# Samples' attention scores on VectorE alone, with their softmax queued behind the prompt's scores

## The chip, the cores and the metric

The kernel runs on one core of a Trainium2 chip. The metric is the device time of one execution in microseconds (us); runs of the kernel before are summed up by their median. Besides them there is one profiled execution with its trace. The engines are named as in the profile: PE (TensorE, matrix products; PEld its weight loads), DVE (VectorE), ACT (ScalarE), POOL (GpSimd) and SP (SyncE, which here only issues transfers). Each engine works through its own queue in order and waits at an instruction whose inputs or buffers aren't ready.

## The reference

One inference step of a decoder layer for a prompt of 1024 rows and 8 samples of 4 rows each, with shared weights, 1024 features wide:

```
p = rmsnorm(x) @ w_in  ->  h, c, b | u, v | q | gate logits gA, gB, gM
y_a = b * conv3(c * h)
y_b = u * spatial_gate(layernorm(v))
y_m = softmax(q k^T / 16) v          (4 heads of 256, 256 memory tokens)
x = x + (sig(gA) y_a + sig(gB) y_b + sig(gM) y_m) @ w_o
x = x + (silu(g) * a) @ w_down,      a, g = conv3(rmsnorm(x) @ w_up) + bias
```

and a last norm. For the prompt all rows share one memory, whose keys and values come from the step itself. Each of the 8 samples has a memory of its own in a cache: 256 keys and 256 values for each head. So the samples' scores are, in each head, 32 rows of q (8 samples of 4), each against the 256 keys of its own sample. This part is what the change touches.

## The kernel before

All 1056 rows lie as columns, features on the partitions. Each weight tile of 128 output features is a *unit*: it is loaded by SP (`load_unit`, L177), split into a rounded high part by ACT (`wh`, L199) and a low rest by DVE (`wl`, L201), and multiplied in three passes (L222 to L224) over three *chunks* of 352 columns. A chunk is 8 x 3 matmuls into one PSUM bank of three (`bank("mm")`), and its evacuation (`evac`) empties the bank with ACT or DVE.

The order is written out by hand. Smaller work stands as a list of functions in the queue `aux`. In every chunk `weave()` is called twice, in its middle and behind its evacuation; each call stands for a *piece* of the large product and emits as many items of `aux` as `pace(n)` spreads over n pieces. What an item emits goes into the queues of its engines at that place.

The attention runs head by head. `plan[h]` lists a head's units: q twice, then h, c, b, h, c, b (the convolution branch; c's evacuation has DVE's convolution at L1127, L316, L318, b's one DVE product at L1137), then u, gB, gA and gM in pairs. At the third unit the list of `att_items(h)` is put into `aux` and paced over 62 pieces; it has 83 items, and heads 1 to 3 get four more (two loads six places before the end, two uses behind it). Head 0 has the rest of the spatial gate's items in the queue ahead of it. At gM the queue is emptied.

The list before, in order:

- `rows`: the 32 rows of q are transposed by PE (L834), copied to `qr` and stored to DRAM (`q_d`). `fetch_q` reads four rows of a sample back on all 128 partitions; `fetch` loads keys or values of two samples from the cache. Buffers come from `fs` (nine slots, F32) and `rs` (eight slots), handed out in turn.
- for each sample `bb` and half of its keys `mt`: `product` (POOL, L852) multiplies the four rows with 128 keys into a buffer of 4 x 256, and `total` (DVE, L865), emitted ahead of the next product, sums it to four columns of `sc`.
- then `masked` (POOL clears two masks), `kv_load` (SP loads the prompt's keys and values of the head), `softmax` (PE transposes `sc` at L874; DVE and ACT normalise), `masked_p`; then for each sample `parts` (its values split) and `against` (its matmuls).
- the prompt at the end: `kv_split` (ACT the high part, L974, DVE the low part, L975), and `score`, `turn_p`, `value` for four tiles of 256 rows: score matmuls at L988 to L990, the maximum at L993, the exponential at L996, transposes at L1013.

The items change places by their order in this list alone; engines and waits follow from it.

Of the kernel before, what the change touches and what calls it, by code (L numbers as in the profile page):

```python
# [9 lines left out]
F32 = mybir.dt.float32  # L10
# [5 lines left out]
P = 128  # L16
# [15 lines left out]
class Slots:  # L32
    """Fixed SBUF buffers of one dtype, handed out in turn."""
# [22 lines left out]
def layer_step(ctx: ExitStack, tc: tile.TileContext, I, O):  # L56
# [52 lines left out]
    def pace(n):  # L109
        """The queued work is to be spread over the next n pieces."""  # L110
        slots_left[0] = n
        due[0] = 0.0

    def until(ready):
        """What is queued, up to the work that makes ready() true."""
        while not ready():
            aux.popleft()()
# [65 lines left out]
    def split_lows():  # L183
        """The low parts, queued apart from the high ones that they wait for."""
        while lows:
            lows.pop()()
# [57 lines left out]
    def rsqrt(ms, out, tmp, n):  # L244
        """out = ms ** -0.5, the square root's table refined by one Newton step."""
        nc.scalar.activation(out=out[:n], in_=ms[:n], func=AF.Sqrt)
        nc.vector.reciprocal(out=out[:n], in_=out[:n])
        nc.vector.tensor_tensor(out=tmp[:n], in0=out[:n], in1=out[:n], op=ALU.mult)
        nc.vector.scalar_tensor_tensor(
            out=tmp[:n], in0=tmp[:n], scalar=-0.5, in1=ms[:n], op0=ALU.mult, op1=ALU.mult  # L250
        )
        nc.vector.scalar_tensor_tensor(
            out=out[:n], in0=tmp[:n], scalar=1.5, in1=out[:n], op0=ALU.add, op1=ALU.mult
        )

    def column_norm(c, g, sums):
        """S's chunk c of columns times their inverse root mean square and g, split into zhi and zlo."""
        r = slice(c * CH, (c + 1) * CH)
        ms, t, y = (small.tile([P, 3], F32, name=n, tag=n, bufs=2) for n in ("ms3", "tmp3", "y3"))
        tmp = fs.get()  # L260
        rows = []

        def total():
            sums(ms)
            nc.vector.tensor_scalar(out=ms, in0=ms, scalar1=1.0 / D, scalar2=EPS, op0=ALU.mult, op1=ALU.add)
            rsqrt(ms, y, t, P)

        def spread():
            b = bank()
            for i in range(3):  # L270
                n = PIECES[3 * c + i][1]
                mmul(
                    b[:, i * P : i * P + n], lhsT=y[:n, i : i + 1].to_broadcast([n, P]), rhs=ident[:n, :n],
                    start=True, stop=True,
                )
            rows.append(b)

        def scale(f):
            def go():
                z = tmp[:, (f % 3) * CH : (f % 3 + 1) * CH]  # L280
                nc.vector.scalar_tensor_tensor(
                    out=z, in0=S[:, f, r], scalar=col(g + f), in1=rows[0][:, :CH], op0=ALU.mult, op1=ALU.mult
                )
                nc.scalar.copy(out=zhi[:, f, r], in_=z)
                if f:
                    low(f - 1)
                if f == 7:
                    low(7)
                    fs.put(tmp)
            return go  # L290

        def low(f):
            z = tmp[:, (f % 3) * CH : (f % 3 + 1) * CH]
            eng = nc.gpsimd if f % 2 else nc.vector
            eng.tensor_tensor(out=zlo[:, f, r], in0=z, in1=f32(zhi[:, f, r]), op=ALU.subtract)  # L295

        nc.gpsimd.memset(ms, 1.0)
        return total, spread, [scale(f) for f in range(8)]
# [4 lines left out]
    def segments(c, hb, o):  # L303
        """(a chunk's columns of o, the function of a tap that gives hb's columns)."""
        t0, t1 = c * CH, min((c + 1) * CH, NP)
        segs = [(o[:, t0:t1], lambda k: hb[:, t0 + k : t1 + k])]
        if c == 2:
            hs = hb[:, 1026:HB].rearrange("p (b x) -> p b x", x=6)
            segs.append((o[:, NP:T].rearrange("p (b x) -> p b x", x=4), lambda k: hs[:, :, k : k + 4]))
        return segs  # L310

    def conv(c, hb, o, w0, step, first=True):
        """A chunk of the causal depthwise convolution of three taps."""
# [22 lines left out]
    def hb_parts(c, hb, ps):  # L336
        """(destination in hb, source in ps) of a chunk's columns."""
# [17 lines left out]
    def tail_rows(src, i0, cnt, prompt, sample):  # L355
        """Rows of the convolution states from their columns, for cnt tiles of channels."""
# [10 lines left out]
    with tc.manual_schedule():  # L367
# [87 lines left out]
        def x_prep(c, copy):  # L455
            """The sums of the squares, by rows; the turns, by columns; the norm's steps."""
# [34 lines left out]
        # mem's parts: 8 x 256 columns in two buffers each  # L491
        class Two:
            """[P, 8, 256] over two buffers."""
# [43 lines left out]
        def prep_sg2(g):  # L537
            def go():
# [7 lines left out]
                # the first 4 x 4 block, transposed, once for each sample on the diagonal  # L546
# [152 lines left out]
        def keep_warm(n):  # L699
            """Products that nothing reads: the tensor engine's clock is halved while it idles."""  # L700
            b = bank("acc")
            for _ in range(n):
                mmul(b[:, :P], lhsT=ident, rhs=ident, start=True, stop=True)
# [59 lines left out]
        kv = {}  # L763

        def turn_k(q):
            """Four tiles of the keys' columns, transposed."""
# [55 lines left out]
        att = {}  # L822

        def att_items(h):
# [5 lines left out]
            # the samples' scores: each row of q, on all partitions, times its memory's keys  # L830
            def rows():
# [3 lines left out]
                qr = small.tile([32, 256], F32, name="qr", tag="qr", bufs=1)  # L835
                nc.scalar.copy(out=qr, in_=b[:32, :256])
                nc.scalar.dma_start(out=q_d[h], in_=qr)
# [10 lines left out]
            def product(bb, mt):  # L848
                def go():
                    t = v3(att["st", bb // 2], 4, 256)  # L850
                    pr = att["pr", bb, mt] = fs.get()
                    nc.gpsimd.tensor_tensor(  # L852
                        out=v3(pr, 4, 256), in0=v3(att["qb", bb], 4, 256),
                        in1=t[:, 2 * (bb % 2) + mt, :].unsqueeze(1).to_broadcast([P, 4, 256]), op=ALU.mult,
                    )
# [4 lines left out]
                return go  # L860

            def total(bb, mt):
                def go():
                    pr = att.pop(("pr", bb, mt))
                    nc.vector.tensor_reduce(  # L865
                        out=att["sc"][:, mt, 4 * bb : 4 * bb + 4], in_=v3(pr, 4, 256), axis=AX.X, op=ALU.add
                    )
                    fs.put(pr)
                return go
# [15 lines left out]
            # their values: all their rows of a head at once, each against its own memory  # L885
# [60 lines left out]

            def folded_o():
                ym[:] = [fs.get(), fs.get()]
# [12 lines left out]
            # the prompt  # L961
# [83 lines left out]
            last = no  # L1045
            for bb in range(8):
                for mt in range(2):
                    items += [lambda last=last, do=product(bb, mt): (last(), do())]
                    last = total(bb, mt)
                    if mt and bb + 2 < 8:  # L1050
                        items.append(fetch_q(bb + 2))
                    else:
                        items.append(no)
                if bb % 2 and bb // 2 + 2 < 4:
                    items.append(fetch(kc, bb // 2 + 2))
            items += [last, masked, fetch(vc, 0), kv_load, softmax, fetch(vc, 1), no, masked_p]
# [6 lines left out]
            items += [against(7), copied, kv_split, folded_o]  # L1063
            items += [score(0), score(1), turn_p(0), score(2), turn_p(1), value(0), score(3), turn_p(2)]
            items += [value(1), turn_p(3), value(2), value(3)]
            return items

# [224 lines left out]
        def down(w, q, j0, nk, fi, r):  # L1292
            """One tile of features of w_down's product over nk tiles of j, added to S."""
# [59 lines left out]
        def finish(a0, a1, end):  # L1353
            """The rows of the columns from a0 to a1: their turns, one by one, then the last steps."""
# [114 lines left out]
```

## Time and profile before

| | |
|---|---|
| time, median of 3 runs | 1937.43 us (1936.9 to 1938.99) |
| span of the profiled execution, first to last instruction | 1939.3 us |
| busy: PE / PEld | 1889.9 / 1865.7 us |
| busy: DVE / ACT / POOL | 1062.2 / 660.5 / 284.7 us |
| mean granted PE clock | 0.988 |

The runs list no time for the profiled execution outside its span. A busy time is a union of spans. A row of a group reads: line, engine, operation, output <- inputs, shape, count | busy us, mean ns of one | idle us of the engine just before them, and what ended it. A row of waits reads: who waited <- for whom: us in total, times, longest. A row of the timeline: start us, length us, engine, line, operation; several of a kind in a row are merged (x2). A row of a stage table: stretch, its length, then busy us and instructions (x) of PE, PEld, DVE, ACT and POOL, the granted clock, the DMA engines' share and GB/s.

### The profile page before, as it was taken

The page shows a single profiled execution, that of the slowest core. Times are in us where ns is not written, and L with a number is a line of the kernel's source. Part 1 is how long each engine was busy: PE and PEld are TensorE (multiplying, and loading weights), DVE is VectorE, ACT ScalarE, POOL GpSimd, SP SyncE. Part 2 cuts the span into 40 slices and gives each one's busy share as a digit, 9 for nine tenths or more (in the row PEclk, how much of TensorE's full clock was granted, in tenths as well). Part 3 has the DMA queues.
Part 4 walks back from the last instruction along what each step waited for, and adds up shares of the span by engine and source line. Part 5 has one row for each costly group of instructions (what it writes and reads, how often), then busy time and mean ns, then how long its engine had stood idle before and what let it go on. Part 6 is the DMA issues. An engine that isn't in the chain of part 4 may idle for free.

```text
span 1939.3 us, 28762 instructions
## 1 busy us (share of the span) xinstructions
PE 1889.9 (97%) x11844; PEld 1865.7 (96%) x11844; DVE 1062.2 (55%) x1826; ACT 660.5 (34%) x1253; POOL 284.7 (15%) x386
## 2 busy tenths in 40 slices
PE   8999998999899989999999999999999999999998
PEld 8988998999899989999899999999999999999997
DVE  4476675336733383327636257636636546546666
ACT  6654312411152113421154135414414314222443
POOL 2231153005300260007100221000000000000000
PEclk9999999999999999999999999999999999999999
DMA  8636144124311252124314201111111111111123
GB/s 259 199 107 214 60 141 132 33 66 135 106 36 45 92 155 62 42 70 140 98 35 138 74 12 34 56 51 49 46 44 44 45 44 44 57 44 44 46 77 134
DMA packets 204848, 160.43 MB, mean 83 GB/s; under 512 B 5477, under 2 KB 191405, under 8 KB 204717
## 3 DMA queue, kind: packets, MB, share of 16 engines
q1 hardware_dynamic: 194660, 144.76, 24.6%
q10 hardware_dynamic: 10057, 13.84, 2.1%
q8 instruction: 93, 1.52, 0.3%
q14 instruction: 38, 0.31, 0.1%
HBM read 144.98 MB, written 13.59 MB: 82 GB/s over the span
## 4 chain that ended last, share of the span: by engine, by line
PE 81%; DVE 10%; issue 4%; ACT 2%; POOL 2%; DMA 1%; ACTq 0%; DVEq 0%; SPq 0%; POOLq 0%
PE mm L222 25%; PE mm L223 25%; PE mm L224 25%; DVE fs L318 3%; DVE sc L865 2%; POOL fs L852 1%; DVE wl L201 1%; DVE fs L316 1%; PE acc L919 1%; ACT wh L199 1%; DVE fs L1127 0%; DMA ws<-in_w_in 0%; PE mm L803 0%; PE aux L989 0%; PE aux L990 0%
## 5 line engine op out<-in xcount | busy, mean ns | idle before, releaser
L222 PE MATMUL mm<-zhi,wh 128*128 128x352 f32 x2880 | 939.8, 326 | 8.6 <-DVE fs L1137 8.3
L223 PE MATMUL mm<-zlo,wh 128*128 128x352 f32 x2880 | 935.4, 325 | 1.0 <-POOL zlo L295 1.0
L224 PE MATMUL mm<-zhi,wl 128*128 128x352 f32 x2880 | 934.9, 325 | 0.0
L222 PEld LDWEIGHTS mm<-zhi,wh 128*128 128x128 f32 x2880 | 546.3, 190 | 11.0 <-issue 7.3
L223 PEld LDWEIGHTS mm<-zlo,wh 128*128 128x128 f32 x2880 | 545.8, 190 | 1.6 <-POOL zlo L295 1.6
L224 PEld LDWEIGHTS mm<-zhi,wl 128*128 128x128 f32 x2880 | 545.9, 190 | 0.1
L201 DVE TENSOR_TENSOR wl<-ws,wh 128x1024 fp32r<-128x1024 f32 x181 | 234.9, 1299 | 141.5 <-ACT wh L199 141.3
L199 ACT CAST wh<-ws 128x1024 fp32r<-128x1024 f32 x182 | 190.9, 1051 | 352.2 <-PE mm L223 298.3
L318 DVE SCALAR_TENSOR_TENSOR fs<-fs,vec,fs 128x352 f32<-128x352 f32 (+2 forms) x416 | 236.5, 582 | 98.2 <-ACT fs L1280 88.9
L852 POOL TENSOR_TENSOR fs<-fs,fs 128x1024 f32<-128x1024 f32 x64 | 161.8, 2550 | 238.6 <-DMA fs<-q_d 204.9
L222 PE MATMUL mm<-rs,wh 128*128 128x352 f32 (+3 forms) x528 | 172.0, 326 | 2.1 <-DVE S L1302 2.1
L223 PE MATMUL mm<-rs,wh 128*128 128x352 f32 (+3 forms) x528 | 171.1, 324 | 0.0
L224 PE MATMUL mm<-rs,wl 128*128 128x352 f32 (+3 forms) x528 | 170.9, 324 | 0.0
L1302 DVE TENSOR_TENSOR S<-mm,S 128x352 f32<-128x352 f32 (+3 forms) x144 | 75.1, 524 | 124.0 <-PE mm L224 123.8
L222 PEld LDWEIGHTS mm<-rs,wh 128*128 128x128 f32 x528 | 99.1, 188 | 3.2 <-ACT fs L360 1.7
L330 POOL COPY tail_f<-fs 128x2 f32<-128x2 f32 x40 | 9.9, 247 | 624.7 <-ACT fs L1279 624.7
L223 PEld LDWEIGHTS mm<-rs,wh 128*128 128x128 f32 x528 | 99.3, 188 | 0.5 <-DVE rs L1269 0.3
L224 PEld LDWEIGHTS mm<-rs,wl 128*128 128x128 f32 x528 | 99.0, 188 | 0.2
L1279 ACT COPY fs<-mm 128x352 f32<-128x352 f32 (+2 forms) x176 | 62.1, 380 | 91.9 <-PE mm L224 85.2
L865 DVE TENSOR_REDUCE sc<-fs 128x4 f32<-128x1024 f32 x64 | 77.3, 1213 | 17.7 <-POOL fs L852 17.7
L1280 ACT ACTIVATE fs<-mm,vec 128x352 f32<-128x352 f32 x132 | 86.5, 656 | 0.0
L1160 DVE TENSOR_TENSOR sig<-sig,fs 128x352 f32<-128x352 f32 x48 | 25.2, 525 | 111.1 <-ACT sig L1147 111.1
(236 smaller groups left out, 1631.3 us busy)
## 6 DMA issues: line engine op xcount, KB each, us to landing
ws<-in_w_in SPq DMA_DIRECT2D x88, 512.0 KB
ws<-in_w_up SPq DMA_DIRECT2D x44, 512.0 KB
fs<-q_d SPq DMA_DIRECT2D x32, 512.0 KB
ws<-in_w_down SPq DMA_DIRECT2D x30, 512.0 KB
fs<-in_cache_mem_k SPq DMA_DIRECT2D x16, 512.0 KB
fs<-in_cache_mem_v SPq DMA_DIRECT2D x16, 512.0 KB
xT_d<-S ACTq DMA_DIRECT2D x3, 1408.0 KB
S<-xT_d ACTq DMA_DIRECT2D x6, 704.0 KB
```

The lines of the kernel that those rows point to most:

```text
L199: nc.scalar.copy(out=hi, in_=t)
L201: lows.append(lambda: eng.tensor_tensor(out=lo, in0=t, in1=f32(hi), op=ALU.subtract))
L222: mmul(ps, lhsT=wh, rhs=xh, start=first, stop=False)
L223: mmul(ps, lhsT=wh, rhs=xl, start=False, stop=False)
L224: mmul(ps, lhsT=wl, rhs=xh, start=False, stop=last)
L318: nc.vector.scalar_tensor_tensor(out=dst, in0=src(k), scalar=col(w0 + k * step), in1=dst, op0=ALU.mult, op1=ALU.add)
L852: nc.gpsimd.tensor_tensor(out=v3(pr, 4, 256), in0=v3(att["qb", bb], 4, 256), in1=t[:, 2 * (bb % 2) + mt, :].unsqueeze(1).to_broadcast([P, ...
L865: nc.vector.tensor_reduce(out=att["sc"][:, mt, 4 * bb : 4 * bb + 4], in_=v3(pr, 4, 256), axis=AX.X, op=ALU.add)
L1160: nc.vector.tensor_tensor(out=t, in0=t, in1=src[:, r], op=ALU.mult)
L1279: nc.scalar.copy(out=dst, in_=src)
L1280: nc.scalar.activation(out=o[:, r], in_=ps, func=AF.Identity, scale=col(CFW + 88 + i), bias=col(CFB + i))
L1302: nc.vector.tensor_tensor(out=S[:, f, r], in0=ps, in1=S[:, f, r], op=ALU.add)
```

## The change

`product` no longer runs on POOL. It emits four DVE instructions, one for each row of q, that multiply 256 elements of the row with 128 keys and sum along the row in the same instruction; the sum goes to one column of `sc`, the product itself to `qr`, enlarged to 128 partitions, which nobody reads after its store. `total` and its buffers are gone.

The list is in another order. `kv_load` stands after the seventh sample's products; behind the last product come `kv_split`, `started` (it takes the two output buffers that `folded_o` took) and the prompt's tiles; `softmax` stands among these, ten items behind the last product; `fetch` of the values, `masked` and `masked_p` follow, then the samples' values as before. It has 83 items again. Other parts of the diff only remove comments.

```diff
-                qr = small.tile([32, 256], F32, name="qr", tag="qr", bufs=1)
-                nc.scalar.copy(out=qr, in_=b[:32, :256])
-                nc.scalar.dma_start(out=q_d[h], in_=qr)
+                att["qr"] = qr = small.tile([P, 256], F32, name="qr", tag="qr", bufs=1)
+                nc.scalar.copy(out=qr[:32], in_=b[:32, :256])
+                nc.scalar.dma_start(out=q_d[h], in_=qr[:32])
...
             def product(bb, mt):
+
                 def go():
                     t = v3(att["st", bb // 2], 4, 256)
-                    pr = att["pr", bb, mt] = fs.get()
-                    nc.gpsimd.tensor_tensor(
-                        out=v3(pr, 4, 256), in0=v3(att["qb", bb], 4, 256),
-                        in1=t[:, 2 * (bb % 2) + mt, :].unsqueeze(1).to_broadcast([P, 4, 256]), op=ALU.mult,
-                    )
+                    q = v3(att["qb", bb], 4, 256)
+                    for i in range(4):
+                        at = 4 * bb + i
+                        nc.vector.tensor_tensor_reduce(
+                            out=att["qr"], in0=q[:, i, :], in1=t[:, 2 * (bb % 2) + mt, :], scale=1.0, scalar=0.0,
+                            op0=ALU.mult, op1=ALU.add, accum_out=att["sc"][:, mt, at : at + 1],
+                        )
...
-            def total(bb, mt):
-                def go():
-                    pr = att.pop(("pr", bb, mt))
-                    nc.vector.tensor_reduce(
-                        out=att["sc"][:, mt, 4 * bb : 4 * bb + 4], in_=v3(pr, 4, 256), axis=AX.X, op=ALU.add
-                    )
-                    fs.put(pr)
-                return go
...
+            def started():
+                ym[:] = [fs.get(), fs.get()]
+
             def folded_o():
-                ym[:] = [fs.get(), fs.get()]
...
-            last = no
             for bb in range(8):
                 for mt in range(2):
-                    items += [lambda last=last, do=product(bb, mt): (last(), do())]
-                    last = total(bb, mt)
-                    if mt and bb + 2 < 8:
-                        items.append(fetch_q(bb + 2))
-                    else:
-                        items.append(no)
+                    items.append(product(bb, mt))
+                    items.append(fetch_q(bb + 2) if mt and bb + 2 < 8 else no)
                 if bb % 2 and bb // 2 + 2 < 4:
                     items.append(fetch(kc, bb // 2 + 2))
-            items += [last, masked, fetch(vc, 0), kv_load, softmax, fetch(vc, 1), no, masked_p]
+                if bb == 6:
+                    items.append(kv_load)
+            items += [kv_split, started, score(0), score(1), turn_p(0), score(2), turn_p(1), value(0), score(3), turn_p(2)]
+            items += [softmax, value(1), turn_p(3), fetch(vc, 0), value(2), value(3), masked, fetch(vc, 1), masked_p]
             for bb in range(8):
...
-            items += [against(7), copied, kv_split, folded_o]
-            items += [score(0), score(1), turn_p(0), score(2), turn_p(1), value(0), score(3), turn_p(2)]
-            items += [value(1), turn_p(3), value(2), value(3)]
+            items += [against(7), copied, no, folded_o]
             return items
```

## The prediction

> **What bounds the kernel now.** I read the page first: TensorE (PE) is busy nearly throughout, so only time in which it waits, or runs at a lowered clock, can be won.
>
> ```profile
> span 1939.3 us, 28762 instructions
> PE 1889.9 (97%) x11844; PEld 1865.7 (96%) x11844; DVE 1062.2 (55%) x1826; ACT 660.5 (34%) x1253; POOL 284.7 (15%) x386
> L852 POOL TENSOR_TENSOR fs<-fs,fs 128x1024 f32<-128x1024 f32 x64 | 161.8, 2550 | 238.6 <-DMA fs<-q_d 204.9
> L865 DVE TENSOR_REDUCE sc<-fs 128x4 f32<-128x1024 f32 x64 | 77.3, 1213 | 17.7 <-POOL fs L852 17.7
> ```
>
> Then the waits in the four heads (244 to 1100 us), by engine and line, and one of them in the timeline:
>
> ```profile
> PE aux L874 <- DVE sc L865: 19.9, 8, 3.8
> 509.38 0.39 PE L874 MATMUL aux<-ident,sc 128*32 128x128 f32 x1 [3.84 <-DVE sc L865]
> 511.64 0.40 PE L874 MATMUL aux<-ident,sc 128*32 128x128 f32 x1 [1.87 <-DVE sc L865]
> L222 PE MATMUL mm<-zhi,wh 128*128 128x352 f32 x1532 | 501.9, 328 | 8.3 <-DVE fs L1137 8.3
> ```
>
> PE waits twice per head: at softmax's transposes (L874), for the last sums of the samples' scores, and once earlier, for a PSUM bank that VectorE (DVE) empties late. What these cost, clock included, is read from the stage table: 480 to 500 us is undisturbed, the other rows hold the stalls.
>
> ```profile
> 290.00:300.00 10.00, 8.34 (x52) 8.08 (x51) 8.47 (x12) 1.05 (x1) 7.13 (x4) 1.00 0.72 218
> 305.00:318.00 13.00, 7.93 (x33) 7.19 (x33) 8.16 (x11) 3.08 (x5) 6.28 (x4) 0.74 0.72 224
> 472.00:478.00 6.00, 3.85 (x24) 3.59 (x23) 6.00 (x8) 1.05 (x1) 3.93 (x2) 1.00 0.83 264
> 480.00:500.00 20.00, 20.00 (x127) 20.00 (x126) 16.36 (x13) 2.91 (x4) 17.82 (x9) 1.00 0.53 157
> 504.00:516.00 12.00, 6.29 (x31) 5.71 (x30) 9.15 (x13) 1.84 (x3) 3.58 (x3) 0.72 0.54 173
> 684.00:694.00 10.00, 7.83 (x39) 7.57 (x39) 9.93 (x14) 1.50 (x2) 6.68 (x3) 0.83 0.64 186
> 720.00:732.00 12.00, 7.50 (x34) 6.68 (x33) 7.41 (x14) 2.03 (x4) 1.10 (x2) 0.72 0.56 175
> 898.00:908.00 10.00, 7.83 (x40) 7.57 (x39) 9.93 (x14) 1.39 (x2) 6.50 (x4) 0.83 0.59 182
> 934.00:946.00 12.00, 7.39 (x33) 6.65 (x31) 7.10 (x13) 1.84 (x3) 1.34 (x2) 0.72 0.56 174
> ```
>
> Undisturbed, PE starts 127/20 = 6.35 matmuls per us, so a chunk (24) takes 3.78 us and a piece (12) 1.89 us. The four softmax windows hold 33, 31, 34 and 33 where 49 us would hold 311: (311 - 131)/6.35 = 28.3 us lost, of which 49 - 29.1 = 19.9 is idleness and 8.4, about 2 per head, is the granted clock (0.72 to 0.74). The four bank windows hold 155 where 36 us would hold 229: 11.6 us. Together **39.9 us** can be won, no more.
>
> Why DVE is late: beside GpSimd (POOL) its convolution steps are slow. The first five rows are the heads, the next three 1120 to 1300 us, where no product runs:
>
> ```profile
> L201 DVE TENSOR_TENSOR wl<-ws,wh 128x1024 fp32r<-128x1024 f32 x64 | 86.5, 1351 | 57.5 <-ACT wh L199 57.4
> L318 DVE SCALAR_TENSOR_TENSOR fs<-fs,vec,fs 128x352 f32<-128x352 f32 x30 | 33.5, 1116 | 1.6
> L318 DVE SCALAR_TENSOR_TENSOR fs<-fs,vec,fs 128x320 f32<-128x320 f32 x16 | 30.1, 1879 | 0.6
> L318 DVE SCALAR_TENSOR_TENSOR fs<-fs,vec,fs 128x32 f32<-128x32 f32 x16 | 4.0, 252 | 0.6
> L1161 DVE TENSOR_TENSOR S<-S,sig 128x352 f32<-128x352 f32 x48 | 25.2, 525 | 1.6
> ...
> L318 DVE SCALAR_TENSOR_TENSOR fs<-fs,vec,fs 128x352 f32<-128x352 f32 x36 | 20.8, 584 | 11.6 <-ACT fs L1280 10.8
> L201 DVE TENSOR_TENSOR wl<-ws,wh 128x1024 fp32r<-128x1024 f32 x13 | 15.9, 1221 | 6.9 <-ACT wh L199 6.9
> L318 DVE SCALAR_TENSOR_TENSOR fs<-fs,vec,fs 128x320 f32<-128x320 f32 x18 | 9.9, 550 | 3.5 <-ACT fs L1280 3.2
> ```
>
> 30 x (1116 - 584) + 16 x (1879 - 550) + 64 x (1351 - 1221) ns = 45.5 us of DVE time, 11.4 a head, is such slowing.
>
> **The change, part by part.** *Removed:* POOL's 16 products a head, the slowing, and DVE's 16 sums (19.4 us a head at 1213 ns). *Added:* 64 multiply-and-sum instructions a head of 128x256, all on DVE. Before shows none. Nearest rows, and how instructions follow one another:
>
> ```profile
> L676 DVE TENSOR_TENSOR S<-aux,S 128x256 f32<-128x256 f32 x32 | 13.6, 425 | 1.1
> L1374 DVE TENSOR_TENSOR ms<-ss 128x1 f32<-128x1 f32 x8 | 1.2, 154 | 1.5 <-ACT fs L1369 1.5
> 499.25 0.51 DVE L1127 TENSOR_TENSOR fs<-mm,fs 128x352 f32<-128x352 f32 x1
> 499.80 0.40 DVE L316 TENSOR_SCALAR fs<-fs,vec 128x352 f32<-128x352 f32 x1
> 500.24 1.21 DVE L318 SCALAR_TENSOR_TENSOR fs<-fs,vec,fs 128x352 f32<-128x352 f32 x2
> 501.36 1.22 DVE L865 TENSOR_REDUCE sc<-fs 128x4 f32<-128x1024 f32 x1
> 6.44 1.06 ACT L464 ACTIVATE S<-fs 128x1024 f32<-128x1024 f32 x1
> 7.41 0.19 ACT L464 ACTIVATION_READ_ACCUMULATOR S<-fs 128x1 f32 x1
> 7.66 1.06 ACT L464 ACTIVATE S<-fs 96x1024 f32<-96x1024 f32 x1
> ```
>
> An independent successor starts 0.09 us before its predecessor's end (501.36 against 501.45), a dependent one 0.04 after it. All 64 write the same tile qr, which nobody reads; ACT's three squares at L464 do the same with S, and there each starts only when the one before, with its accumulator read, is over: 7.66 - 6.44 = 1.22, or 0.16 us beyond the main duration. So for the time t from start to start: at the least 0.425 - 0.09 = 0.34 (nothing waits, no read); 0.46 (dependent, no read); 0.34 + 0.154 + 0.04 = 0.53 (a read like DVE's smallest operation); 0.425 + 0.16 = 0.585 (ACT's overhead). I take **t = 0.50**, between the two middle ones, and keep 0.34 and 0.585 for the range.
>
> [...]
>
> *What the new work delays.* DVE works in order. In the stretch of the products it also has to empty PE's banks, split the weights, and now, right after the last product, split the prompt's keys (kv_split), for which the prompt's first score matmul waits. Head 1, from these starts:
>
> ```profile
> 439.36 0.38 PE L834 MATMUL aux<-ident,qs 128*32 128x128 f32 x2
> 450.82 1.23 DVE L201 TENSOR_TENSOR wl<-ws,wh 128x1024 fp32r<-128x1024 f32 x1 [10.43 <-ACT wh L199]
> 446.18 4.78 POOL L852 TENSOR_TENSOR fs<-fs,fs 128x1024 f32<-128x1024 f32 x2 [64.57 <-DMA fs<-q_d]
> 441.71 0.81 SPq L843 DMA_DIRECT2D fs<-q_d  x2
> ```
>
> The first product stands behind the weight split that ends at 452.05 (q has landed by 446.18, so that wait is hidden by 5.9 us). Behind it, up to the end of kv_split: 64t; the c units' chunks, 4 x 2.11 (499.25 to 501.36) and 2 last ones of about 2.9 (320 and 32 columns apart); 4 of b's chunks at 0.45; 4 weight splits at 1.15; kv_split's low half 1.22. That is 21.9 + 64t: DVE is through at 474.0 + 64t. PE's due time: the list has 87 items for 62 pieces, 1.40 a piece; score(0) is the 46th, so piece 33, 32 pieces after the transposes: 439.5 + 32 x 1.89 = 500.0. **The new wait is 64t - 26.0**, 6.0 us at t = 0.50; about 2 remain even with a cheap t, since kv_split stands behind the last c chunk, which itself waits for PE. With 2 us for the clock, as above: 8.0 a head. Head 0 starts with what is left of the spatial gate, so its list is denser but one c unit falls out of the stretch; I take it equal. Banks: DVE is at most some 6 us late with one, and three banks allow two chunks, 7.6.
>
> *Moved, costed at nothing:* softmax, ten items after the last product: its sums are long done. The prompt's scores, turns and values come during b and u; they are the same instructions, and in the heads their turns never waited:
>
> ```profile
> L1013 PE MATMUL aux<-ident,fs 128*128 128x128 f32 x64 | 9.6, 272 | 0.0
> SPq L843 <- DVE sc L865: 115.5, 13, 20.0
> ```
>
> The two items between a score and its turn cover that chain; if b's evacuations took the cover it would be under 1 us a tile. On SP, kv_load's two loads now stand behind the last fetch of q and ahead of the values of the cache, which move behind the prompt; no POOL product holds buffers any more, so the waits of q's fetches for a buffer (second row) mostly go. The masks' memsets meet an empty POOL.
>
> **Sum:** -39.9 + 4 x 8.0 = -7.9 us on the span of 1939.3, which stands 1.9 above the median of the runs, with nothing around it shown. On the median of 1937.43: **1929.5 us**. The same sum at the ends: t = 0.34 gives -39.9 + 4 x 2 = -32, 1905; t = 0.585 gives -39.9 + 4 x (11.4 + 2) = +14, 1951.
>
> **Rivals.** (1) *Multiply-and-sum is cheap*, t up to 0.46: wait 3.4 + 1.5 or less: 1905 to 1917. For: with immediate scalars it looks like L676. Against: ACT's reads.
> (2) *The wait only moves*: L874's wait goes, the score matmuls of the prompt wait as long. That is 64t - 26.0 + 2 = 39.9/4, t = 0.53: within 0.2% (3.9 us, about what these runs can tell from no change) for t of 0.52 to 0.55: 1937.
> (3) *Slower: DVE becomes the bound of the product stretch.* Place: kv_split behind the 64th product. From t = 0.55 on each 0.01 us costs 4 x 0.64 = 2.6 us: 1942 at 0.55, 1951 at 0.585, 1960 at 0.62. For: a chain of 64 waits, ACT's 0.16. Against: DVE's smallest instructions are shorter than ACT's read.
> [...]
> (5) *Late q*: DVE itself now waits for q's transfers, and the emptying of PE's banks and the weight splits queue behind that wait, with PE behind them (the transfer takes 4.5 us from 441.71 to 446.18; each is issued three pieces, 5.7 us, ahead of its product). Late by 2 us in each head: +8, 1937.
>
> **Chances.** Forecast (t 0.46 to 0.52) 0.36; (1) 0.22; (2) 0.11; (3) 0.20; (4) 0.05; (5) 0.06. Faster: 0.36 + 0.22 = 0.58; same: 0.11 and half of (5), 0.14; slower: the rest, 0.28. The range takes in the bounds of t and some of (3): 1905 to 1957; the forecast's own is 1917 to 1934.
>
> **What would show it.** POOL's L852 and DVE's sums gone; L318 in the heads at 0.58 us; multiply-and-sums starting 0.50 us apart; L874 without wait; PE's wait, 6 us a head, now at the prompt's score matmul for the keys' low half. Wrong would be: that wait absent or above 10 us, a wait of DVE for q, or bank waits still there.

## The result, and the profile after

The changed kernel takes 1911.8 us (median of 4 runs, 1910.7 to 1912.2); the kernel before, beside it, 1938.2. The ratio is 0.986, with a 95% interval of 0.9846 to 0.9874: 26.4 us faster, more than three times the 7.9 us forecast and inside the range. (One execution of e4 below, the profiled one, took 3740.2 us, with matmuls of 535 instead of 324 ns; the comparison leaves it out, and e4b repeats that kernel for its profile.)

The first lines of the changed kernel's page:

```profile
span 1910.1 us, 29127 instructions
PE 1878.9 (98%) x11844; PEld 1856.4 (97%) x11844; DVE 1040.7 (54%) x2274; ACT 631.7 (33%) x1231; POOL 123.8 (6%) x322
```

The groups of its DVE work in the heads (244 to 1080 us):

```profile
L855 DVE CUSTOM_DVE_ANT_0 qr<-fs,fs 128x256 f32<-128x256 f32 x256 | 108.5, 424 | 7.3
L855 DVE DVE_READ_ACCUMULATOR2_ANT sc<- 128x1 f32 x256 | 21.0, 82 | 0.0
L318 DVE SCALAR_TENSOR_TENSOR fs<-fs,vec,fs 128x352 f32<-128x352 f32 x28 | 16.4, 585 | 1.5
L318 DVE SCALAR_TENSOR_TENSOR fs<-fs,vec,fs 128x320 f32<-128x320 f32 x16 | 8.8, 552 | 0.6
L201 DVE TENSOR_TENSOR wl<-ws,wh 128x1024 fp32r<-128x1024 f32 x64 | 78.2, 1222 | 64.8 <-ACT wh L199 64.7
```

POOL's products and DVE's sums are gone, and with them the slowing: the convolution steps are back at 585 and 552 ns, from 1116 and 1879. The multiply-and-sum shows as two instructions: the main one (CUSTOM_DVE_ANT_0), 424 ns, and a read of its accumulator, 82 ns. In the waits of the heads neither softmax's transposes nor a bank of the product is left; one PE wait is:

```profile
PE aux L985 <- DVE rs L971: 10.2, 4, 3.8
```

That is the prompt's first score matmul with the keys' low half (L971, kv_split), as forecast, but 10.2 us in all. The four places as stages (columns as before: PE, PEld, DVE, ACT, POOL busy, granted clock, DMA share, GB/s):

```profile
296.00:308.00 12.00, 8.20 (x47) 7.96 (x46) 7.97 (x25) 1.02 (x4) 0.00 (x0) 0.86 0.15 44
490.00:502.00 12.00, 9.86 (x58) 9.61 (x58) 7.58 (x21) 2.09 (x5) 0.00 (x0) 0.86 0.15 45
697.00:709.00 12.00, 9.86 (x68) 9.61 (x68) 8.50 (x22) 2.42 (x7) 0.00 (x0) 1.00 0.15 44
903.00:915.00 12.00, 9.87 (x58) 9.62 (x57) 7.67 (x21) 2.20 (x5) 0.00 (x0) 0.86 0.15 44
```

Head 0 idles 3.8 us, the others 2.14; in three of the four the clock is lowered for a while afterwards (0.86).

### The profile page after: what moved, and what is told of

Same layout as the page of the kernel before. It is cut to its first block, busy times and chain, and to the rows that moved or that the text cites. A ratio compares the mean times of both kernels' runs of the same rounds, so it can differ in the third digit from the quotient of the medians.

```text
span 1910.1 us, 29127 instructions
## 1 busy us (share of the span) xinstructions
PE 1878.9 (98%) x11844; PEld 1856.4 (97%) x11844; DVE 1040.7 (54%) x2274; ACT 631.7 (33%) x1231; POOL 123.8 (6%) x322
## 4 chain that ended last, share of the span: by engine, by line
PE 86%; DVE 7%; issue 3%; ACT 2%; DMA 0%; POOL 0%; DVEq 0%; ACTq 0%; POOLq 0%
PE mm L224 26%; PE mm L222 26%; PE mm L223 26%; DVE qr L855 2%; DVE wl L201 1%; DVE fs L318 1%; PE acc L913 1%; ACT wh L199 1%; PE aux L985 0%; PE aux L986 0%; PE mm L803 0%; PE aux L223 0%; PE aux L984 0%; PE aux L222 0%; PE aux L224 0%
## 5 line engine op out<-in xcount | busy, mean ns | idle before, releaser
L201 DVE TENSOR_TENSOR wl<-ws,wh 128x1024 fp32r<-128x1024 f32 x181 | 226.6, 1253 | 146.7 <-ACT wh L199 146.5
L318 DVE SCALAR_TENSOR_TENSOR fs<-fs,vec,fs 128x352 f32<-128x352 f32 (+2 forms) x416 | 199.4, 492 | 98.6 <-ACT fs L1272 88.8
L855 DVE CUSTOM_DVE_ANT_0 qr<-fs,fs 128x256 f32<-128x256 f32 x256 | 108.5, 424 | 7.3
L1139 ACT ACTIVATE sig<-mm 128x352 f32<-128x352 f32 x72 | 33.5, 465 | 187.7 <-PE mm L224 187.3
L1280 ACT ACTIVATE fs<-fs 128x352 f32<-128x352 f32 x66 | 32.9, 498 | 98.2 <-DVE fs L318 98.1
```

Of the source, the lines that this page charges most:

```text
L201: lows.append(lambda: eng.tensor_tensor(out=lo, in0=t, in1=f32(hi), op=ALU.subtract))
L318: nc.vector.scalar_tensor_tensor(out=dst, in0=src(k), scalar=col(w0 + k * step), in1=dst, op0=ALU.mult, op1=ALU.add)
L855: nc.vector.tensor_tensor_reduce(out=att["qr"], in0=q[:, i, :], in1=t[:, 2 * (bb % 2) + mt, :], scale=1.0, scalar=0.0, op0=ALU.mult, op1=A ...
L1139: nc.scalar.activation(out=t, in_=ps, func=AF.Sigmoid)
L1280: nc.scalar.activation(out=hold["s"][:, r], in_=o[:, r], func=AF.Sigmoid)
```

## Experiments

The theory after the result: the DVE instruction with POOL's silence wins everything that can be won, and the new order costs something, namely the one wait that is left. Rivals: the order is what removed softmax's wait; DVE was late before because it waited for POOL's products, not because it was slowed.

All edits are against the changed kernel. Each ratio is to the kernel before as it ran beside that kernel (its medians lie between 1938.2 and 1938.6 us). "Over e3" is the time above that of e3, the one kernel in which PE doesn't wait in the heads at all.

| kernel | time, us | ratio to before (95%) | PE's waits in the heads, us | over e3, us |
|---|---|---|---|---|
| before | 1938.2 | 1 | 28.2 | 41.6 |
| changed | 1911.8 | 0.986 (0.9846 to 0.9874) | 10.2 | 15.2 |
| e1 DVE sums, old order | 1898.2 | 0.979 (0.9779 to 0.9805) | 1.3 | 1.6 |
| e2 new order, POOL products | 1949.5 | 1.006 (1.0044 to 1.0071) | 40.2 | 52.9 |
| e3 keys split earlier | 1896.6 | 0.978 (0.977 to 0.9797) | 0 | 0 |
| e5 one product more | 1940.6 | 1.001 (1.0003 to 1.0021) | 34.0 | 44.0 |
| e6 POOL products beside | 2028.2 | 1.046 (1.0443 to 1.0485) | 106.2 | 131.6 |
| e4 half of the products in place | 1902.9 | 0.982 (0.9804 to 0.9836) | 5.4 (e4b) | 6.3 |
| e7 in place and PSUM | 1907.2 | 0.984 (0.9823 to 0.9855) | 7.3 | 10.6 |
| e8 four places each | 1900.7 | 0.981 (0.9791 to 0.9824) | 3.6 | 4.1 |

**e1: one part alone.** The list goes back to the order of before; the DVE instruction stays.

```diff
-            items += [kv_split, started, score(0), score(1), ...]
-            items += [softmax, value(1), turn_p(3), fetch(vc, 0), ...]
+            items += [no, masked, fetch(vc, 0), kv_load, softmax, fetch(vc, 1), no, masked_p]
...
-            items += [against(7), copied, no, folded_o]
+            items += [against(7), copied, kv_split, lambda: (started(), folded_o())]
+            items += [score(0), score(1), turn_p(0), score(2), turn_p(1), value(0), score(3), turn_p(2)]
+            items += [value(1), turn_p(3), value(2), value(3)]
```

> The multiply-and-sum on DVE as in the changed kernel, but the list in the order of the kernel before (softmax four items behind the last product, the prompt's tiles at the end). Theory: the whole gain comes from the DVE instruction, and the new order only adds the wait for the low half of the prompt's keys. In the changed kernel a head's last product ended 61.1 us after the transposes of q; in this order PE reaches softmax's transposes at the 47th item, piece 34, 33 x 1.91 = 63.2 us after them. So no wait at softmax, none for the keys: about 10 us of idle time and 3 of clock less than the changed kernel's 1911.8, that is 1899 to 1903 us, no PE wait over 1 us in the heads. Rival (the order is needed): softmax's transposes wait 2 to 4 us a head again and the time is that of the changed kernel or worse, 1911 to 1925.

Measured 1898.2 us, 13.6 us below the changed kernel and just under the range expected. The only PE wait of its heads:

```profile
PE aux L868 <- DVE sc L855: 1.3, 1, 1.3
```

Softmax behind the last product, where it stood, waits only once, in head 0 (1.3 us, where no wait over 1 us was expected). So softmax didn't need to move, and the new order as it stands costs 13.6 us. What in it costs them, e3 tells.

**e2: the other part alone.** The new order with POOL's products and DVE's sums.

```diff
...
-                    items.append(product(bb, mt))
+                    items.append(lambda last=last, do=product(bb, mt): (last(), do()))
+                    last = total(bb, mt)
...
-            items += [kv_split, started, ...]
+            items += [lambda last=last: (last(), kv_split()), started, ...]
```

> The new order alone: GpSimd's products and DVE's sums as in the kernel before, the last sum directly ahead of the split of the prompt's keys. Theory: the convolution steps are slowed again (L318 128x352 over 1.0 us instead of 0.585), the bank wait of 2 to 4 us a head is back, softmax waits no more, but the prompt's first score matmul waits for the keys' split, which stands behind the last sum on DVE: last sum 72 us after q's transposes in the kernel before, PE due at about 65, so 7 to 10 us a head. Time 1938 to 1955. Rival (the order is what won the time): no more than 1925.

1949.5 us, 11 us slower than before. PE's waits in the heads:

```profile
PE aux L991 <- DVE rs L977: 31.6, 4, 8.5
PE mm L222 <- DVE fs L1137: 8.6, 4, 2.5
```

Two of its groups there:

```profile
L318 DVE SCALAR_TENSOR_TENSOR fs<-fs,vec,fs 128x320 f32<-128x320 f32 x16 | 30.0, 1873 | 0.6
L318 DVE SCALAR_TENSOR_TENSOR fs<-fs,vec,fs 128x352 f32<-128x352 f32 x28 | 26.4, 943 | 1.5
```

The slowed steps and the bank wait (8.6 us) are back, and in place of softmax's 19.9 us PE now waits 31.6 for the keys. The order alone doesn't remove a wait; it exchanges it for an earlier and longer one. (L318 at 352 columns came out at 943 ns, not over 1 us.)

**e3: the wait that is left, taken away.** The keys are loaded a sample earlier and split ahead of the last sample's products.

```diff
-                if bb == 6:
+                if bb == 5:
                     items.append(kv_load)
-            items += [kv_split, started, score(0), ...]
+                if bb == 6:
+                    items.append(kv_split)
+            items += [started, score(0), ...]
```

> The changed kernel with the load of the prompt's keys one sample earlier and their split ahead of the last sample's products. Theory: the only PE wait of the changed kernel's heads, 10.2 us in four waits for the keys' low half, and the lowered clock behind three of them are gone: 1899 to 1903 us. Rival (DVE is so far behind at this place that PE's banks or the scores' maxima make PE wait instead): a wait of 2 to 4 us a head at another line, 1909 to 1913.

1896.6 us, faster than the kernel before, the changed kernel and e1, and 2.4 us below the range expected. The heads in one stage:

```profile
240.00:1065.00 825.00, 825.00 (x5301) 820.70 (x5301) 414.56 (x1061) 206.45 (x392) 25.24 (x49) 1.00 0.30 94
```

PE is busy in all 825 us at full clock. DVE carries the same 64 multiply-and-sums a head, so DVE's load as such isn't what costs time; what stands behind the products and is needed next does. Softmax stands here where the new order put it, so the loss of that order lies in the place of the keys' split. It also gives a yardstick: the changed kernel's 15.2 us above e3 are 10.2 us of waiting and 5.0 us that no wait shows, 1.25 us a head. The lowered clock accounts for them: three of the four stages above stand at 0.86 over 12 us, and 3 x 0.14 x 12 = 5.0 us.

**e5: more of the same work.** The first multiply-and-sum of each product is done twice, 16 more a head.

```diff
-                    for i in range(4):
+                    for i in (0, 0, 1, 2, 3):
```

> The changed kernel with five instead of four multiply-and-sums in each product (the first is done twice), 16 more a head at 0.468 us. Theory (the wait for the keys' low half is what is left of DVE's work in this stretch, 64 x 0.468 + 21.9 us against PE's due time): DVE has 1.2 us of idle time in the stretch of head 1, so the wait grows by 6.3 to 7.5 us a head, from 2.1 to about 9; with the clock 26 to 38 us more, 1938 to 1950. Rival (the products run in DVE's idle time and the wait comes from somewhere else): under 1920.

1940.6 us: 28.8 us more than the changed kernel for 16 x 0.468 = 7.5 us of DVE work a head, or 30 us in four. Its waits:

```profile
PE aux L985 <- DVE rs L971: 32.8, 4, 8.4
PE mm L222 <- DVE fs L1129: 1.2, 2, 0.8
```

The same wait grows by 22.6 us, 5.7 a head, a little under the 6.3 expected; the rest is clock and two short bank waits. Beyond what would be left with cheap products, the wait is DVE's backlog of products, the work that it still has to do when PE comes for the keys. At t = 0.585 for 64, as the upper end of the forecast had it, the same 7.5 us a head would have come from dearer instructions: this kernel stands for that case, and comes out 0.1% above the time of before.

**e6: POOL's products, unread, beside DVE's.**

```diff
+                    pr = fs.get()
+                    nc.gpsimd.tensor_tensor(
+                        out=v3(pr, 4, 256), in0=q,
+                        in1=t[:, 2 * (bb % 2) + mt, :].unsqueeze(1).to_broadcast([P, 4, 256]), op=ALU.mult,
+                    )
+                    fs.put(pr)
```

> The changed kernel, with GpSimd's 64 products of the kernel before run beside it into buffers that nobody reads. DVE's own instructions are those of the changed kernel. Theory (DVE's two-input instructions are held up while GpSimd reads SBUF): L318 128x352 rises from 0.585 to about 1 us and 128x320 from 0.55 to 1.9, and some multiply-and-sums take 2 to 3 us; at the least the 11 us a head of slowing that the kernel before had come back, all of it in the wait for the keys' low half: over 1955 us. Rival (DVE was late in the kernel before because its sums waited for GpSimd's products, not because it was slowed): durations as in the changed kernel, 1911 to 1916.

2028.2 us. Groups of DVE in the heads:

```profile
L861 DVE CUSTOM_DVE_ANT_0 qr<-fs,fs 128x256 f32<-128x256 f32 x256 | 182.5, 713 | 7.3
L318 DVE SCALAR_TENSOR_TENSOR fs<-fs,vec,fs 128x320 f32<-128x320 f32 x16 | 29.8, 1862 | 0.6
L318 DVE SCALAR_TENSOR_TENSOR fs<-fs,vec,fs 128x32 f32<-128x32 f32 x16 | 20.0, 1247 | 1.1
L318 DVE SCALAR_TENSOR_TENSOR fs<-fs,vec,fs 128x352 f32<-128x352 f32 x28 | 16.4, 585 | 1.5
```

and PE's waits there:

```profile
PE mm L222 <- DVE fs L1135: 45.7, 4, 11.8
PE aux L991 <- DVE rs L977: 35.1, 4, 9.1
PE mm L222 <- DVE fs L1125: 25.4, 5, 5.8
```

Nothing on DVE reads what POOL makes here, and still the multiply-and-sums rise from 424 to 713 ns and L318 at 320 and 32 columns from 552 and 252 to 1862 and 1247: about (713 - 424) x 256 + (1862 - 552) x 16 + (1247 - 252) x 16 ns = 111 us over four heads. The timeline shows the single instructions, DVE's first, then POOL's beside them:

```profile
512.93 2.62 DVE L861 CUSTOM_DVE_ANT_0 qr<-fs,fs 128x256 f32<-128x256 f32 x1
515.60 2.50 DVE L861 CUSTOM_DVE_ANT_0 qr<-fs,fs 128x256 f32<-128x256 f32 x1
511.96 8.40 POOL L854 TENSOR_TENSOR fs<-fs,fs 128x1024 f32<-128x1024 f32 x3 [8.30 <-DVE sc L861]
```

By the trace 37 of the 256 multiply-and-sums ran beside a product of POOL. Of these 35 took 2.4 to 2.65 us, and the two that had begun ahead of POOL's product took 0.42, like the rest. DVE is slowed by POOL itself, and the rival falls. The kernel before shows the same in head 1, two L318 beside three products of POOL:

```profile
493.03 5.17 DVE L318 SCALAR_TENSOR_TENSOR fs<-fs,vec,fs 128x352 f32<-128x352 f32 x2
490.33 7.49 POOL L852 TENSOR_TENSOR fs<-fs,fs 128x1024 f32<-128x1024 f32 x3
```

By its trace each of the 18 L318 beside L852 took 2.53 to 2.73 us, and every other one of 352 or 320 columns at most 0.59. "Two-input instructions" in the expectation's theory is too wide: L1137, with one of its two inputs in PSUM, took 0.51 to 0.53 us beside L852 (13 times) as elsewhere, and L865, with one input, 1.20 to 1.22 (35 times). Whether POOL's reading or its writing does it, no run here tells apart. My picture of which instructions are hit was wrong in one place: L318 at 352 columns stays at 585, and by the trace none of its 28 ran beside a product of POOL here.

**e4, e4b, e7, e8: what one multiply-and-sum costs.** In the changed kernel's timeline four of them run so:

```profile
443.23 1.23 DVE L201 TENSOR_TENSOR wl<-ws,wh 128x1024 fp32r<-128x1024 f32 x1 [10.43 <-ACT wh L199]
444.37 0.42 DVE L855 CUSTOM_DVE_ANT_0 qr<-fs,fs 128x256 f32<-128x256 f32 x1
444.71 0.09 DVE L855 DVE_READ_ACCUMULATOR2_ANT sc<- 128x1 f32 x1
444.83 0.42 DVE L855 CUSTOM_DVE_ANT_0 qr<-fs,fs 128x256 f32<-128x256 f32 x1
445.18 0.08 DVE L855 DVE_READ_ACCUMULATOR2_ANT sc<- 128x1 f32 x1
445.30 0.42 DVE L855 CUSTOM_DVE_ANT_0 qr<-fs,fs 128x256 f32<-128x256 f32 x1
```

0.47 us from start to start: the read begins 0.34 to 0.35 after the main instruction, takes 0.08, and the next one starts 0.04 after that. e4 lets the second half of the keys write its unread products over the rows of q:

```diff
+                        if mt:
+                            nc.vector.tensor_tensor_reduce(
+                                out=q[:, i, :], in0=q[:, i, :], in1=t[:, 2 * (bb % 2) + mt, :], scale=1.0, scalar=0.0,
+                                op0=ALU.mult, op1=ALU.add, accum_out=att["sc"][:, mt, at : at + 1],
+                            )
```

> The changed kernel, but for the second half of each sample's keys the unread product goes over the row of q itself (four different places) instead of all into qr; the first half writes qr as before. Theory: the 35 ns of idle time ahead of every multiply-and-sum, and the loss of the 0.08 us overlap, come from all of them writing one tile, each waiting for the accumulator read before it; so the second half's start to start falls from 0.468 to about 0.42 (main instruction to read 0.34, read 0.08) with no idle time between, the first half's stays at 0.468. 32 x 0.04 = 1.3 us a head less of DVE work, the wait for the keys' low half about 1 us shorter a head: 1903 to 1908 us. Rival (the gap belongs to the accumulator read itself): both halves at 0.468, time 1911 to 1913.

> The kernel with the second half's unread products in place once more, for a profile at full clock. Expected from its time of 1902.9 us: the first half's multiply-and-sums 0.468 us apart, the second half's 0.346, so a mean of 0.407, and 32 x 0.122 = 3.9 us a head less DVE work than in the changed kernel; the wait for the keys' low half 0 to 1.5 us a head.

1902.9 and 1902.4 us, 9 us below the changed kernel and just under e4's range. The two groups of e4b (L856 in place, L861 into qr):

```profile
L861 DVE CUSTOM_DVE_ANT_0 qr<-fs,fs 128x256 f32<-128x256 f32 x128 | 54.1, 423 | 3.3
L856 DVE CUSTOM_DVE_ANT_0 fs<-fs,fs 128x256 f32<-128x256 f32 x128 | 46.6, 419 | 0.0
```

and its PE wait in the heads:

```profile
PE aux L991 <- DVE rs L977: 5.4, 4, 1.4
```

In place there is no idle time before an instruction, and the second half's instructions start 0.346 us apart by the trace, as e4b's expectation had it. The gain per instruction is three times the 0.04 us that I expected at first, 0.12; the timeline of e8 below shows it. e7 sends the first half's products to two halves of a free PSUM bank in turn, e8 to four places of a free buffer; the second half stays in place.

```diff
-                            out=att["qr"], in0=q[:, i, :], ...
+                            out=q[:, i, :] if mt else att["unread"][:, i % 2 * 256 : (i % 2 + 1) * 256], in0=q[:, i, :], ...
```

> The changed kernel in its own order, no multiply-and-sum writing a place that the one before wrote: the second half's products in place, the first half's in two halves of a free PSUM bank in turn. Theory: all 64 a head about 0.35 us apart, 7.8 us of DVE time less a head. The wait for the keys' low half goes only to its floor: behind the last c chunk stand its evacuation (2.9), the last product (1.4), a weight split (1.15), one bank (0.45) and the split itself (1.2), 7.1 us, and PE is due three pieces, 5.7 us, behind that chunk: 1 to 1.5 us a head, no lowered clock: 1900 to 1903 us. Rival (the wait is DVE's whole backlog and goes with it): no PE wait in the heads, 1896 to 1898 us.

1907.2 us, not 1900 to 1903. Its groups:

```profile
L857 DVE CUSTOM_DVE_ANT_0 acc<-fs,fs 128x256 f32<-128x256 f32 x128 | 55.2, 431 | 3.3
L857 DVE CUSTOM_DVE_ANT_0 fs<-fs,fs 128x256 f32<-128x256 f32 x128 | 46.6, 419 | 0.0
L857 DVE DVE_READ_ACCUMULATOR2_ANT sc<- 128x1 f32 x256 | 28.3, 111 | 0.0
```

and its PE wait:

```profile
PE aux L988 <- DVE rs L974: 7.3, 4, 2.1
```

Two halves of one bank didn't act as two places: the idle time is still there, and the reads are longer on average (111 ns instead of 82). Whether the shared bank or PSUM as such does this was not tried. So e7 doesn't settle what would be left of the wait with cheap products.

```diff
+                    pr = None if mt else fs.get()
+                    o = q if mt else v3(pr, 4, 256)
...
-                            out=att["qr"], in0=q[:, i, :], ...
+                            out=o[:, i, :], in0=q[:, i, :], ...
```

> The changed kernel in its own order, the first half's unread products in four places of a free buffer, the second half's in place: no two neighbours write the same tile's place. Theory: all 64 a head 0.346 us apart without idle time (the second half measured that, the first half was held at 0.468 by qr and at 0.52 by the PSUM bank), 7.8 us of DVE time a head less than in the changed kernel. The wait for the keys' low half nevertheless stays near 1.35 us a head, where it stood with half of them at 0.346, less at most the 0.5 us of the last product, since it now goes by when PE ends the last c chunk: 0.9 to 1.4 us a head, 1901 to 1903 us. Rival (it is all backlog): no PE wait, 1896 to 1898 us.

1900.7 us, just under the range expected. A piece of DVE's timeline:

```profile
452.46 0.42 DVE L857 CUSTOM_DVE_ANT_0 fs<-fs,fs 128x256 f32<-128x256 f32 x1
452.81 0.08 DVE L857 DVE_READ_ACCUMULATOR2_ANT sc<- 128x1 f32 x1
452.81 0.42 DVE L857 CUSTOM_DVE_ANT_0 fs<-fs,fs 128x256 f32<-128x256 f32 x1
453.15 0.08 DVE L857 DVE_READ_ACCUMULATOR2_ANT sc<- 128x1 f32 x1
```

and the PE wait in the heads:

```profile
PE aux L989 <- DVE rs L975: 3.6, 3, 1.2
```

Now 0.35 us apart: the read lies beside the next main instruction and costs nothing, so 0.12 us of each 0.47 came from the shared unread tile. And with 64 x 0.122 = 7.8 us a head less DVE work, 1.2 us of the wait remain in three heads (the forecast had about 2). In head 1:

```profile
482.09 0.59 DVE L1123 TENSOR_TENSOR fs<-mm,fs 128x320 f32<-128x320 f32 x2 [0.26 <-PE mm L224]
487.85 1.22 DVE L975 TENSOR_TENSOR rs<-fs,rs 128x1024 fp32r<-128x1024 f32 x1
489.12 0.39 PE L989 MATMUL aux<-rs,rs 128*128 128x256 f32 x1 [1.19 <-DVE rs L975]
```

DVE had caught up: it sat idle for 0.26 us until PE was through with the last c chunk (L1123 is its evacuation). From there to the end of the keys' split it took 489.07 - 482.09 = 7.0 us, and PE was free for them at 489.12 - 1.19 = 487.93. So this part of the wait isn't backlog. e3, which moves the split, removes it with the dear instructions still in place.

## Why the prediction was wrong

The mechanism held step by step: the two old waits went, the slowing went (585 ns against 584 forecast), the new wait appeared where it was said to, behind kv_split, and DVE waited nowhere for q's transfers. What failed is the sizes of four terms of the sum, all to one side, the time of one multiply-and-sum and the new wait above all. From -7.9 to -26.4 us:

1. **"I take t = 0.50"**: measured 0.468. The model behind the third candidate was right (dependent on the one before, with a read of its own), but I priced the read at DVE's smallest operation with inputs, 0.154; it took 0.082. 4 x 64 x 0.032 = 8.2 us.
2. **"The new wait is 64t - 26.0"**: at t = 0.468 that gives 3.95 a head, and 2.55 was measured on average (10.2/4): 5.6 us. In heads 1 to 3 it was 2.14, 1.8 less than the formula gives. DVE's side was good: from the end of the weight split at 444.46 (443.23 + 1.23) to the end of kv_split at 495.87 (below) it took 51.4 us, where 21.9 + 64 x 0.468 gives 51.9. PE's due time was most of the miss. DVE's and PE's timelines of the changed kernel's head 1:

```profile
493.07 1.22 DVE L201 TENSOR_TENSOR wl<-ws,wh 128x1024 fp32r<-128x1024 f32 x1
494.21 0.52 DVE L1129 TENSOR_TENSOR fs<-mm,fs 128x352 f32<-128x352 f32 x1
494.65 1.22 DVE L971 TENSOR_TENSOR rs<-fs,rs 128x1024 fp32r<-128x1024 f32 x1
```

```profile
431.77 0.38 PE L834 MATMUL aux<-ident,qs 128*32 128x128 f32 x2
493.17 0.32 PE L223 MATMUL mm<-zlo,wh 128*128 128x352 f32 x1
493.33 0.32 PE L224 MATMUL mm<-zhi,wl 128*128 128x352 f32 x1
493.49 0.28 PE L984 MATMUL aux<-rs,rs 128*128 128x256 f32 x1
495.92 0.39 PE L985 MATMUL aux<-rs,rs 128*128 128x256 f32 x1 [2.15 <-DVE rs L971]
```

   DVE is in the first, PE in the second. PE reached the keys 61.7 us after the transposes of q (493.49 - 431.77), not 60.5, and it still had L984's 0.28 us to run before it waited. Matmuls start 0.16 us apart (493.17, 493.33, 493.49). The forecast's 127 in 20 us, 0.157 apart, counted two that only reach over the stage's edge (by the trace 125 start in it); over 384 matmuls this makes 1 us, and a wait that is a difference of two times near 60 us changes by a quarter. Head 0, "I take it equal", isn't: PE came for its keys 50.2 us after the transposes (298.25 - 248.05 in the trace). That its 3.8 us lie close to the formula's 3.95 is chance.
3. **"2 us for the clock"** a head: 5.0 us in all, 1.25 a head, by what is left over e3 and by the stages' clock alike. The forecast had 2.1 from each of the old softmax windows; now three waits paid about 1.7 and one nothing. 3.0 us.
4. **"39.9 us can be won"**: 41.6 by e3: 1.7 us, the same edge effect. Counted by starts alone, the forecast's eight windows (85 us) hold 270 matmuls by the trace before, and at 125 in 20 us, 6.25 per us, 85 - 270/6.25 = 41.8.

These sum to 18.5 us, the whole miss. The rivals: (1) comes nearest: its 1905 to 1917 us hold the measured time, but by luck. Its condition, t up to 0.46, isn't met; at the measured t, inside the forecast's own 0.46 to 0.52, the forecast's sum gives 1937.4 - 39.9 + 4 x 5.95 = 1921.3, and the other three terms made the rest. (2) and (3) were placed right but need t from 0.53, and e5 shows the price that (3) named. (4), a multiply-and-sum dearer still than in (3), rested on nothing that a row or a run shows: with two float32 sources in SBUF and the accumulator in use the instruction took 424 ns, as L676's plain product of the same width did (425). (5) didn't happen.

One question the prediction never asked was whether the order should change at all. By its own working at t = 0.50 the last product ends at 474.0 + 32 - 2.8 = 503.2 (the weight split, the bank and the keys' split, 2.8 us, come after it), and softmax's old place, the 47th item, falls 33 pieces after the transposes, at 501.9: a wait of 1.3 us a head instead of 6.0. The terms were there; the sum for the order left alone was not made.

## What to carry to other kernels

Where a change bundles a cheaper operation with a new order, forecast each alone; here the operation won 40 us (e1) and the order gave 13.6 back. A wait like PE's for the keys (2.14 us in heads 1 to 3) is the difference of two long sums (near 60 us each), so read both rates start to start from the timeline rather than from counts in a stage, and look what stands between the bulk work and the one instruction that the bottleneck needs next: moving that instruction (e3) was worth more than making the bulk a quarter cheaper (e8). In these kernels an output that nobody reads still set the pace of the instructions that write it (0.47 us apart with one tile in the changed kernel); give neighbours different places (four in an SBUF buffer were enough in e8, 0.35 us apart; two halves of a PSUM bank weren't in e7, with 3.3 us of idle time over 128).

## What the runs showed of the hardware

- The accumulator read of the multiply-and-sum is an instruction of its own (82 ns; 83 in e8) and cost nothing in e8, where the next instruction didn't wait for it: 0.35 us apart against 0.47 with one shared unread tile in the changed kernel.
- Two halves of one PSUM bank as unread outputs still gave the idle time of a dependent instruction (3.3 us over 128 in e7), four places in SBUF none (e8; the rows of q in place in e4b and e7, 0.0 us over 128).
- A lowered clock doesn't follow from the length of a wait alone: of three waits of the same 2.13 to 2.15 us in the changed kernel two were followed by it (stages at 490 and 903 us, 0.86) and one was not (697 us, 1.00). Why was not tried.
